# A new opening order with halved weight loads, a column-group mean square, and row additions of the first FFN stage moved ahead

## The chip, the cores and the metric

The kernel runs on one core of a Trainium2 chip. The core has a matrix engine (TensorE, PE in the profile; PEld is its weight load), a vector engine (VectorE, DVE), a scalar engine (ScalarE, ACT), GpSimd (POOL) and SyncE (SP), which here only issues transfers. Each engine works through its own list of instructions in order and waits on semaphores for the others. On-chip memory is SBUF; matmuls write PSUM. The metric is the device time of one execution in microseconds; less is better.

## What is computed

A decoder trunk of two layers over 512 tokens of width 1024. Each layer is a half-step SwiGLU FFN, a token mixer and a second half-step FFN, each behind an RMS norm that is modulated by adaLN columns computed from `c`:

```python
c_act = jax.nn.silu(c)
for l in range(DEPTH):
    mod = (c_act @ w_ada[l] + b_ada[l]).reshape(B, N_MOD, D_MODEL)
    sh1, sc1, gt1, sh2, sc2, gt2, sh3, sc3, gt3 = [mod[:, i, None, :] for i in range(N_MOD)]
    hn = rms_norm(h, g_ffn1[l]) * (1.0 + sc1) + sh1
    h = h + 0.5 * (1.0 + gt1) * swiglu(hn, w_ffn1_in[l], w_ffn1_out[l])
    ...
```

All inputs are float32. The kernel splits each large operand into a high part (rounded to the fast matmul format fp32r) and a low part (the rest), and forms a product as three matmuls: high x high, high x low, low x high.

## The kernel before

**Layout.** The residual `h` lies in SBUF transposed: eight row blocks k = 0 to 7 of 128 features by 512 tokens. A weight tile is 128 output features by 1024 inputs, 512 KB; for output tile n the pair wH, wL (high, low) is made from the raw tile by a copy on ACT and a subtraction on DVE (`split`, L136 to L141; in the opening L1430 and L1432). An output tile of the FFN's input side takes 8 row blocks x 3 matmuls of 128x512 = 24 (`mm3`, L123 to L129).

**The opening** (`begin`, L1317) computes the first norm and its modulation and, interleaved with them, the first six output tiles (n = 0 to 5, gate and up of three pairs) of the first FFN. It runs in a pool of its own, `first`, which holds the adaLN streams (`wada`, 4 buffers of 1 MB), the raw weights (`wfirst`), the scaled rows `z`, and the pairs of tiles 4 and 5; the pairs of tiles 0 to 3 lie in the pool `wp`, which all stages share. Nearly all its instructions are pinned (`pin`, L1324): each engine takes them in the order in which `PLAN` (L33) is walked. A word of `PLAN` is one step:

- `R`: the reciprocal root mean square spread over all partitions (PE); `z`k: h[k] times it (DVE).
- `ada`k, `part`k, `col`k, `gm`k: the scale and shift columns of row block k from stream k, on PE; `d`k and `e`k: the same as two dot products on DVE (L1394), each followed by a read of the accumulator, and `gm`.
- `x`k: z[k] scaled and shifted (ACT, L1422); `H`k and `L`k: high and low part of the normed row block, hnH on ACT, hnL on DVE (L1424, L1426).
- `wH`n, `wL`n: the pair of weight tile n. `W`n: n matmuls on ones whose result nobody reads (warm-up).
- `P`nk and a letter: one large matmul of tile n and row block k (L1409): `a` high weight x hnH, `b` high weight x hnL, `c` low weight x hnH.

The loads of the opening go out on SP in the order of the calls of `fetch` (a stream of 1 MB) and `fetch_w` (a weight tile); `more` (L1396) adds calls after some steps, as buffers come free. Before the plan, ACT and DVE square the eight row blocks, DVE adds the squares in seven steps (L1375), and PE sums over partitions (L1380).

**The first stage** (`ffn`, L350) uses the pool `act`, which takes the place of `first` in SBUF once that is closed. `projector` (L305) yields the opening's six tiles and computes ten more, n = 6 to 15, each with a freshly loaded pair; raw weights have two buffers (`wraw`), pairs four. Of each gate and up tile ACT takes silu, DVE multiplies (L522), ACT and DVE split the result into actH and actL (L523, L524). Meanwhile DVE forms further adaLN columns as dot products with `crep` (silu(c) on all partitions, which the opening writes to memory and this stage loads, L203), and prepares the second half of the stage, which uses a Strassen-like scheme over pairs (`pair_in`): `whole(n)` (L394) adds hnH and hnL of four row blocks back to full values, four additions of 128x512 into tiles `x` of the pool `act`; `combine` (L402) makes the sums P1, P2, T3, T4 of them. `late` (L500) says behind which of the stage's sixteen tiles each of these six steps is put. Apart from the pins a scheduler places the instructions of an engine by the order in which they are written and by when their inputs are ready; `queue_behind(name)` (L133) puts an instruction behind the one kept under that name in the order of its engine.

Of the kernel before, what the change touches and what calls it, by code (L numbers as in the profile page):

```python
# [17 lines left out]
P = 128  # L18
# [14 lines left out]
PLAN = """  # L33
ada0 R0 part0 s0 col0 z0 wH0 ada1 gm0 z5 x0 z4 part1 z1 H0 W2 col1 z7 s1 P00a wH1 gm1 z3 x1 L0 W4 P10a ada2 z6 wH2 z2 H1 P00b wL2 P10b P20a part2 P20b
P01a wH3 col2 L1 P20c P11a gm2 P30a P30b wL3 x2 P01b P11b P21a P21c H2 P21b d3 P31a P30c P31b P31c P02a P12a L2 P22a P22c P32a e3 P02b P12b P22b wH4
P32c P32b wL0 W1 P40a x3 P40b P41a P41b P42a H3 P42b d4 P00c P01c P02c P03a P03c L3 P13a wH5 P23a P23c P33a e4 P03b P13b P50a P50b P51a P51b P52a wL5
x4 P52b P23b P33c P33b H4 P43a d5 P43b P50c P51c P52c P53a P53b L4 P53c P04a P04c e5 P14a P04b P14b P24a P24c P24b P34a P34c wL4 x5 P34b P44a P44b
P54a H5 P54c d6 P54b P40c P41c P42c P43c P44c L5 P05a P05c P15a e6 P05b P15b P25a P25c P25b P35a P35c wL1 P35b x6 P45a P45c P45b P55a H6 P55c d7 P10c
P11c P12c P13c P14c P15c L6 P55b P06a P06c e7 P06b P16a P16c P16b P26a P26c P26b x7 P36a P36c P36b P46a H7 P46c P46b P56a P56c L7 P56b P07a P07c P07b
P17a P17c P17b P27a P27c P27b P37a P37c P37b P47a P47c P47b P57a P57c P57b  # L40
""".split()
GROUPS = ((0, 12), (12, 22))
STEP = 0.65
# [25 lines left out]
def trunk_kernel(ctx, tc, ins, out, layers=L, phases=("ffn1", "mix", "ffn2")):  # L69
# [280 lines left out]
    def ffn(l, w_in, w_pair, w_out, hn, im, ss, need, then, first, ready, coming):  # L350
# [6 lines left out]
        with tc.tile_pool(name="act", bufs=1) as ap_:  # L357
# [36 lines left out]
            def whole(n):  # L394

                for k in (2 * n, 2 * n + 4):
                    x = ap_.tile([P, 2, T], F32, name="x", tag="act", bufs=12)
                    for i in range(2):
                        tt(x[:, i], *(t.bitcast(F32) for t in hn[k + i]), ALU.add)
                    rows_.append(x)  # L400

            def combine(name):  # L402
# [108 lines left out]
            for g, (j0, j1) in enumerate(GROUPS):  # L511
                for p in range(j0 // 2, j1 // 2):
                    if p < n_first:
                        X = new_x(p)
                        for j in (2 * p, 2 * p + 1):
# [4 lines left out]
                            act(pg.like(s), pg.view, AF.Silu)  # L520
                            for seen, part in pu.pieces(s):
                                stt(part, part, -1.0, seen, ALU.mult, ALU.mult)  # L522
                            nc.scalar.copy(xs[j][0], s)  # L523
# [793 lines left out]
    def begin(pool):  # L1317
# [12 lines left out]

        wa, wf = [], []

        def fetch():
            w = pool.tile([P, 2 * D], F32, name="wada", tag="wada", bufs=4)
            nc.sync.dma_start(w, ins["wa0"][len(wa)])
            wa.append(w)

        def fetch_w():
            j, g = divmod(len(wf), 2)
            w = pool.tile([P, KD, P], F32, name="wfirst", tag="wfirst", bufs=5)  # L1340
            nc.sync.dma_start(w, ins["w1i"][0, j, g])
            wf.append(w)

# [15 lines left out]
        for k in range(KD):  # L1359
            pin("PE", mm(turned[k // 4][:, k % 4], cT[:, k : k + 1].to_broadcast([P, P]), cst("ident"), start=True, stop=True))  # L1360
        warm(22)
        ss, sqs = new_ss(), {}
        sqs[0] = ss
        for i in range(KD):
            if i in (3, 4):
                x = pool.tile([P, T], F32, name="sqs", tag=f"sq{i}")
            else:
                x = E("sq") if i else ss
            sqs[i] = x
            if i == 3:  # L1370
                pin("DVE", tt(x, h[i], h[i], ALU.mult))
            else:
                pin("ACT", act(x, h[i], AF.Square))
        for a, b in ((0, 1), (0, 2), (0, 3), (4, 5), (4, 6), (4, 7), (0, 4)):
            pin("DVE", tt(sqs[a], sqs[a], sqs[b], ALU.add))  # L1375
        for f in (fetch, fetch_w, fetch, fetch_w, fetch_w, fetch, fetch_w, fetch):
            f()
        pt = psum([P, NB], "ps_ss")
        for b in range(NB):
            pin("PE", mm(pt[:, b : b + 1], ss[:, b * P : (b + 1) * P], ones[:, :1], start=True, stop=True))  # L1380
        r = pool.tile([P, NB], F32, name="rstd_t", tag="rstd_t")
        pin("ACT", act(r, pt, AF.Sqrt, bias=vals["eps"], scale=1.0 / D))
        pin("DVE", nc.vector.reciprocal(r, r))
        rstd = psum([P, T], "ps_rstd", "r1")
        pin("DVE", stt(col["gb"], bsc, 1.0, g1, ALU.add, ALU.mult))
        zs, ws, part, sums, pts = {}, {}, {}, {}, {}

        def finish(c, sc, sh):
            pin("DVE", stt(col["gm0"][:, c], sc, g1[:, c], col["gb"][:, c], ALU.mult, ALU.add))
            pin("DVE", tt(col["sh0"][:, c], sh, bsh[:, c], ALU.add))  # L1390

# [3 lines left out]

        more = {"ada0": (fetch, fetch_w), "ada1": (fetch,), "wL0": (fetch_w, fetch), "e3": (fetch,)}  # L1396

        def step(token):
            kind = "P" if token[0] == "P" else token.rstrip("0123456789")
            k = token[len(kind) :]  # L1400
            if kind == "W":
                return warm(int(k))
            if kind == "P":
                n, k, p = int(k[0]), int(k[1]), "abc".index(k[2])
                if n not in pts:
                    pts[n] = psum([P, T], "ps_mm", ("r0", "r1", "mm")[n % 3])
                w, x = ws[n][p == 2][:, k], weave(hn[k][p == 1])
                first, last = (token == ends[n][e] for e in range(2))
                latest["large"] = pin("PE", mm(paired(pts[n]), w, x, start=first, stop=last, skip_group_check=True))  # L1409
                return  # L1410
            k = int(k)
            c = slice(k, k + 1)
            if kind == "R":
                for b in range(NB):
                    pin("PE", mm(rstd[:, b * P : (b + 1) * P], r[:, b : b + 1].to_broadcast([P, P]), cst("ident"), start=True, stop=True))
            elif kind == "s":
                pin("ACT", act(crep[:, k * 512 : k * 512 + 512], turned[k].rearrange("p k n -> p (k n)"), AF.Silu))
            if kind == "z":
# [6 lines left out]
            elif kind == "L":  # L1425
                pin("DVE", nc.vector.tensor_sub(hn[k][1], zs[k], hn[k][0].bitcast(F32)))  # L1426
            elif kind == "wH":
                home, bufs = (wp, 4) if k < 4 else (pool, 2)
                ws[k] = tuple(home.tile([P, KD, P], F32R, name=x, tag=x, bufs=bufs) for x in ("wH", "wL"))
                pin("ACT", nc.scalar.copy(ws[k][0], wf[k]))  # L1430
            elif kind == "wL":
                pin("DVE", nc.vector.tensor_sub(ws[k][1], wf[k], ws[k][0].bitcast(F32)))  # L1432
            elif kind == "ada":
# [11 lines left out]
            elif kind == "gm":  # L1445
                finish(c, sums[k][:, :1], sums[k][:, 1:])
            elif kind == "d":
                dot(k, "sc", 0)
            elif kind == "e":
                dot(k, "sh", D)  # L1450
                finish(c, col["sc"][:, c], col["sh"][:, c])
            for f in more.get(token, ()):
                f()

# [41 lines left out]
def lay_out(i):  # L1496
# [11 lines left out]
    streams = first.transpose(3, 1, 0, 2, 4).reshape(KD, P, 2 * D)  # L1508
    a["wa0"] = c(np.concatenate([streams[:3], wT[0, 1::-1, 3:].transpose(1, 2, 0, 3).reshape(5, P, 2 * D)]))
    for n, w in (("w1", "w_ffn1_in"), ("w2", "w_ffn2_in")):  # L1510
# [66 lines left out]
```

## Time and profile before

| | us |
|---|---|
| median of three runs (1805.30 to 1809.03) | 1805.43 |
| the profiled execution, whole | 1807.22 |
| its span, first to last instruction | 1805.5 |
| PE busy in the span | 1774.8 |
| DVE busy | 1350.3 |
| ACT busy | 840.9 |

All times of the profile count from the start of the span. The page gives totals and the costliest groups of instructions. The other views are answers from the same trace: the busy time of each engine by stretches, the timeline of an engine (start, duration, engine, line, operation, output<-inputs, count; in brackets how long the engine was idle before it and what ended that), the waits by pairs, and the transfers by issuing line. A timeline row with a count above 1 is a merged run of alike instructions.

### The profile page before, as it was taken

The page shows a single profiled execution, that of the slowest core. Times are in us where ns is not written, and L with a number is a line of the kernel's source. Part 1 is how long each engine was busy: PE and PEld are TensorE (multiplying, and loading weights), DVE is VectorE, ACT ScalarE, POOL GpSimd, SP SyncE. Part 2 cuts the span into 40 slices and gives each one's busy share as a digit, 9 for nine tenths or more (in the row PEclk, how much of TensorE's full clock was granted, in tenths as well). Part 3 has the DMA queues.
Part 4 walks back from the last instruction along what each step waited for, and adds up shares of the span by engine and source line. Part 5 has one row for each costly group of instructions (what it writes and reads, how often), then busy time and mean ns, then how long its engine had stood idle before and what let it go on. Part 6 is the DMA issues. An engine that isn't in the chain of part 4 may idle for free.

```text
span 1805.5 us, 33687 instructions
## 1 busy us (share of the span) xinstructions
PE 1774.8 (98%) x13848; PEld 1616.9 (90%) x13848; DVE 1350.3 (75%) x2187; ACT 840.9 (47%) x1295; POOL 142.5 (8%) x227
## 2 busy tenths in 40 slices
PE   8999999999999999999999999999999999999999
PEld 6889899987778999899899989999876798999998
DVE  6688587877767977677888776887686788864862
ACT  5353255374443554255355524544654345533541
POOL 0101010101000001100100020110000000010000
PEclk9999999999999999999999999999999999999999
DMA  8667876623123576967737687773421427684742
GB/s 342 218 176 232 243 201 197 228 65 103 54 88 120 150 200 193 291 181 206 246 108 200 180 290 204 195 231 105 122 73 32 141 79 198 186 245 132 198 141 71
DMA packets 91405, 309.93 MB, mean 172 GB/s; under 512 B 10417, under 2 KB 11185, under 8 KB 90225
## 3 DMA queue, kind: packets, MB, share of 16 engines
q1 hardware_dynamic: 61920, 201.58, 32.9%
q0 software_dynamic: 29328, 106.18, 23.5%
q8 instruction: 109, 1.79, 0.4%
q14 instruction: 48, 0.39, 0.1%
HBM read 303.79 MB, written 3.93 MB: 170 GB/s over the span
## 4 chain that ended last, share of the span: by engine, by line
PE 81%; DVE 9%; DMA 4%; ACT 4%; issue 3%; POOL 0%; SPq 0%; ACTq 0%; DVEq 0%; POOLq 0%
PE ps_mm L127 13%; PE ps_mm L128 13%; PE ps_mm L129 13%; PE ps_d L431 7%; PE ps_d L433 7%; PE ps_d L432 7%; PE ps_f L433 3%; PE ps_f L431 3%; PE ps_f L432 3%; PE ps_g L433 2%; PE ps_g L431 2%; PE ps_g L432 2%; DVE wL L141 2%; PE ps_mm L1409 1%; ACT wH L139 1%
## 5 line engine op out<-in xcount | busy, mean ns | idle before, releaser
L139 ACT CAST wH<-wraw 128x1024 fp32r<-128x1024 f32 (+2 forms) x290 | 263.9, 916 | 465.8 <-PE ps_mm L128 212.4
L141 DVE TENSOR_TENSOR wL<-wraw,wH 128x1024 fp32r<-128x1024 f32 (+2 forms) x290 | 305.5, 1058 | 123.3 <-ACT wH L139 122.0
L127 PE MATMUL ps_mm<-actH,wH 128*128 128x512 f32 (+1 forms) x784 | 281.0, 358 | 0.0
L129 PE MATMUL ps_mm<-actH,wL 128*128 128x512 f32 (+1 forms) x784 | 280.6, 358 | 0.3 <-DVE wL L141 0.3
L128 PE MATMUL ps_mm<-actL,wH 128*128 128x512 f32 (+1 forms) x784 | 280.5, 358 | 0.0
L127 PE MATMUL ps_mm<-hnH,wH 128*128 128x512 f32 (+1 forms) x712 | 246.8, 353 | 1.7 <-ACT hnH L289 1.3
L128 PE MATMUL ps_mm<-hnL,wH 128*128 128x512 f32 (+1 forms) x712 | 246.2, 348 | 0.1
L129 PE MATMUL ps_mm<-hnH,wL 128*128 128x512 f32 (+1 forms) x712 | 244.8, 346 | 0.6 <-DVE wL L141 0.6
L431 PE MATMUL ps_d<-comH,wH 128*128 128x256 f32 x816 | 225.2, 276 | 0.8 <-ACT s L457 0.7
L432 PE MATMUL ps_d<-comL,wH 128*128 128x256 f32 x816 | 224.4, 275 | 0.0
L433 PE MATMUL ps_d<-comH,wL 128*128 128x256 f32 x816 | 224.4, 275 | 0.0
L141 DVE TENSOR_TENSOR wL<-sum,wH 128x1024 fp32r<-128x1024 f32 x102 | 124.9, 1225 | 81.0 <-ACT wH L139 80.8
L197 DVE SCALAR_TENSOR_TENSOR wada<-wada,crep 128x1024 f32<-128x1024 f32 x128 | 153.2, 1219 | 29.2 <-DMA wada<-in_wadaT 28.9
L129 PEld LDWEIGHTS ps_mm<-actH,wL 128*128 128x128 f32 x784 | 148.7, 190 | 17.5 <-DVE wL L141 0.7
L127 PEld LDWEIGHTS ps_mm<-actH,wH 128*128 128x128 f32 x784 | 148.7, 190 | 16.8 <-ACT wH L139 0.2
L128 PEld LDWEIGHTS ps_mm<-actL,wH 128*128 128x128 f32 x784 | 148.7, 190 | 16.6
L431 PEld LDWEIGHTS ps_d<-comH,wH 128*128 128x128 f32 x816 | 156.6, 192 | 2.3 <-ACT s L457 2.3
L433 PEld LDWEIGHTS ps_d<-comH,wL 128*128 128x128 f32 x816 | 156.7, 192 | 0.0
L432 PEld LDWEIGHTS ps_d<-comL,wH 128*128 128x128 f32 x816 | 156.6, 192 | 0.0
L139 ACT CAST wH<-sum 128x1024 fp32r<-128x1024 f32 x102 | 106.8, 1047 | 104.6 <-PE ps_f L432 42.4
L127 PEld LDWEIGHTS ps_mm<-hnH,wH 128*128 128x128 f32 x712 | 133.1, 190 | 22.0 <-issue 7.9
L129 PEld LDWEIGHTS ps_mm<-hnH,wL 128*128 128x128 f32 x712 | 135.4, 190 | 14.0 <-DVE wL L141 1.0
(389 smaller groups left out, 3861.0 us busy)
## 6 DMA issues: line engine op xcount, KB each, us to landing
wada<-in_wadaT POOLq DMA_DIRECT2D x128, 512.0 KB, 4.8
wraw<-in_wmi SPq DMA_DIRECT2D x40, 512.0 KB, 3.6
wraw<-in_w2p SPq DMA_DIRECT2D x36, 512.0 KB, 3.8
wraw<-in_w1p SPq DMA_DIRECT2D x32, 512.0 KB, 4.3
wraw<-in_w1o SPq DMA_DIRECT2D x32, 384.0 KB, 4.4
wraw<-in_w2o SPq DMA_DIRECT2D x32, 384.0 KB, 4.6
wraw<-in_w1o SPq DMA_DIRECT2D x32, 320.0 KB, 3.7
wraw<-in_w2o SPq DMA_DIRECT2D x32, 320.0 KB, 3.4
```

The lines of the kernel that those rows point to most:

```text
L127: mm(acc, wH, xH, start=start, stop=False)
L128: mm(acc, wH, xL, start=False, stop=False)
L129: latest["large"] = mm(acc, wL, xH, start=False, stop=stop)
L139: nc.scalar.copy(hi, src)
L141: return nc.vector.tensor_sub(lo, src, hi.bitcast(F32))
L197: stt(w, w, 1.0, crep, ALU.mult, ALU.mult, accum_out=out_)
L431: mm(acc, wH, xH, start=start and i + k == 0, stop=False, skip_group_check=True)
L432: mm(acc, wH, xL, start=False, stop=False, skip_group_check=True)
L433: mm(acc, wL, xH, start=False, stop=k == 3, skip_group_check=True)
L1409: latest["large"] = pin("PE", mm(paired(pts[n]), w, x, start=first, stop=last, skip_group_check=True))
```

## The change

It rewrites the opening and touches the first stage in three places.

1. Each raw weight tile of the opening is loaded and split in two halves of 256 KB (row blocks 0 to 3, and 4 to 7); `wH` and `wL` become steps on a half (`wH1a`, `wL1a`, ...). `fetch` takes a word, and all opening loads are pinned on SP. `wfirst` has six buffers.
2. The silu of `c` is taken before it is spread; `crep` is a plain copy. The squares are summed by PE as they are made: for each row block four matmuls with a 32-column weight of ones, each into its own group of 32 partitions. Of 28 warm-up matmuls ahead of the plan's, 22 go and 8 come.
3. Scale and shift columns are finished on ACT instead of DVE. Stream 2 moves from PE (`ada2`, `part2`, `col2`) to DVE (`d2`, `e2`).
4. `PLAN` is new; the host lays stream 2 out for the dot products.
5. `whole(0)` is called at the start of the stage and its last addition kept as "sums"; wL of tile 6 and the products of the first three pairs are queued behind it. `whole(1)` is put behind tile 1, and the four sums two tiles earlier than before.

```diff
 PLAN = """
-ada0 R0 part0 s0 col0 z0 wH0 ada1 gm0 z5 x0 z4 part1 z1 H0 W2 col1 z7 s1 P00a wH1 gm1 z3 x1 L0 W4 P10a ada2 z6 wH2 z2 H1 P00b wL2 P10b P20a part2 P20b
...
+R0 ada0 z2 wH1a z0 wH3a z6 part0 z7 W2 col0 wL1a gm0 x0 z1 W3 ada1 wL3a H0 z3 wH5a P10a P10c P30a z5 part1 P30c wH0a P50a wL5a col1 wH2a P00a L0 P50c
+gm1 P20a wL2a x1 P00b P10b P20b wL0a P20c H1 P30b P50b d2 P00c P01a P01c P11a P11c L1 P21a P21c P31a wH4a e2 P01b P11b P21b P31c P31b z4 P51a gm2 P51c
+x2 P51b wL4a P40a P40b P41a d3 H2 P40c P41b P41c P02a P02c P12a e3 P12c P22a P22c P32a P32c L2 gm3 P42a P42c x3 P52a d4 P02b P12b P22b H3 P32b P42b e4
...
+P55a x6 P55c wL2b P05b P15b d7 P25b H6 P24c P25c P35b P45b P55b L6 P06a P16a P16c e7 P06b P16b P26a P26c P26b wL0b gm7 P36a P36b x7 P46a wL3b P04c
+P05c P06c H7 P34c P35c P36c L7 P46c P46b P56a P56c P56b P07a P07c P07b P17a P17c P17b P27a P27c P27b P37a P37c P37b P47a P47c P47b P57a P57c P57b
 """.split()
+HALF = {"a": slice(0, KD // 2), "b": slice(KD // 2, KD)}
+BANK = ("r0", "r0", "mm", "r1", "r1", "mm")
...
-            places = {3: ("norm_act", "norm_dve"), 4: ("act", "dve")} if ready else {}
+            places = {3: ("norm_act", "norm_dve"), 4: ("act", "dve")} if ready else {6: (None, "sums")} if pts else {}
...
-            late = ((1, 0), (3, 1), (4, "P1"), (5, "P2"), (6, "T3"), (7, "T4"))
+            late = ((1, 1), (10, "P1"), (11, "P2"), (12, "T3"), (13, "T4"))
             early = ((0, 0), (3, 1), (3, "P1"), (4, "P2"), (5, "T3"), (5, "T4"))
-            when = [(8 + m, n) for m, n in late] if n_first == 4 else early
+            when = late if n_first == 4 else early
+            if n_first == 4:
+                latest["sums"] = whole(0)
...
-                            for seen, part in pu.pieces(s):
-                                stt(part, part, -1.0, seen, ALU.mult, ALU.mult)
+                            with queue_behind("sums" if n_first == 4 and j < 3 else None):
+                                for seen, part in pu.pieces(s):
+                                    stt(part, part, -1.0, seen, ALU.mult, ALU.mult)
...
+        def fetch(token):
+            n = int(token[1])
+            if token[0] == "a":
+                w = wa[n] = pool.tile([P, 2 * D], F32, name="wada", tag="wada", bufs=4)
+                pin("SP", nc.sync.dma_start(w, ins["wa0"][n]))
+            else:
+                if n not in wf:
+                    wf[n] = pool.tile([P, KD, P], F32, name="wfirst", tag="wfirst", bufs=6)
+                pin("SP", nc.sync.dma_start(wf[n][:, HALF[token[2]]], ins["w1i"][0, n // 2, n % 2][:, HALF[token[2]]]))
...
+        pss = psum([P, P], "ps_ss")
+        sqs = {}
         for i in range(KD):
+            sqs[i] = pool.tile([P, T], F32, name="sqs", tag="z", bufs=KD)
+            if i in (3, 5, 7):
+                pin("DVE", tt(sqs[i], h[i], h[i], ALU.mult))
             else:
+                pin("ACT", act(sqs[i], h[i], AF.Square))
+            for b in range(NB):
+                pin("PE", mm(pss[32 * b : 32 * b + 32], ones[:, :32], sqs[i][:, b * P : (b + 1) * P], start=i == 0, stop=i == KD - 1))
...
+        for token in "a0 w1a w3a a1 w5a w0a w2a a2 w4a a3".split():
+            fetch(token)
+        warm(5)
...
         def finish(c, sc, sh):
-            pin("DVE", stt(col["gm0"][:, c], sc, g1[:, c], col["gb"][:, c], ALU.mult, ALU.add))
-            pin("DVE", tt(col["sh0"][:, c], sh, bsh[:, c], ALU.add))
+            pin("ACT", act(col["gm0"][:, c], sc, AF.Identity, bias=col["gb"][:, c], scale=g1[:, c]))
+            pin("ACT", act(col["sh0"][:, c], sh, AF.Identity, bias=bsh[:, c]))
...
-        more = {"ada0": (fetch, fetch_w), "ada1": (fetch,), "wL0": (fetch_w, fetch), "e3": (fetch,)}
+        more = {"ada0": "a4 w5b", "ada1": "a5 w4b w1b w2b", "e2": "a6 w3b w0b", "e3": "a7"}
...
+            if kind in ("wH", "wL"):
+                n, part_ = int(k[0]), HALF[k[1]]
+                if n not in ws:
+                    home, bufs = (wp, 4) if n < 4 else (pool, 2)
+                    ws[n] = tuple(home.tile([P, KD, P], F32R, name=x, tag=x, bufs=bufs) for x in ("wH", "wL"))
+                wH, wL, w = (x[:, part_] for x in (*ws[n], wf[n]))
```

`fetch`, `warm` and `whole` are as shown or described above; `BANK` names the PSUM banks of the six tiles.

More of the change, by code (lines that the diff above doesn't have):

```diff
@@ L398, in whole @@
                     for i in range(2):
-                        tt(x[:, i], *(t.bitcast(F32) for t in hn[k + i]), ALU.add)
+                        last_ = tt(x[:, i], *(t.bitcast(F32) for t in hn[k + i]), ALU.add)
                     rows_.append(x)
+                return last_
             def combine(name):
@@ L1329, in pin @@
             return m
[L1331 to L1342, printed above, removed]
+        wa, wf = {}, {}
+        def fetch(token):
[7 more added lines that the diff above has]
+                pin("SP", nc.sync.dma_start(wf[n][:, HALF[token[2]]], ins["w1i"][0, n // 2, n % 2][:, HALF[token[2]]]))
         pw = psum([P, T], "ps_warm", "mm")
@@ L1359, in begin @@
         for k in range(KD):
[L1360 to L1363, printed above, removed]
+            pin("PE", mm(turned[k // 4][:, k % 4], cact[:, k : k + 1].to_broadcast([P, P]), cst("ident"), start=True, stop=True))
+        pss = psum([P, P], "ps_ss")
+        sqs = {}
         for i in range(KD):
-            if i in (3, 4):
-                x = pool.tile([P, T], F32, name="sqs", tag=f"sq{i}")
-            else:
[L1368 to L1382, printed above, removed]
+            sqs[i] = pool.tile([P, T], F32, name="sqs", tag="z", bufs=KD)
@@ L1383, in begin @@
+            if i in (3, 5):
+                warm((i - 1) // 2)
+        for token in "a0 w1a w3a a1 w5a w0a w2a a2 w4a a3".split():
+            fetch(token)
+        warm(5)
+        r = pool.tile([P, P], F32, name="rstd_t", tag="rstd_t")
+        pin("DVE", stt(col["gb"], bsc, 1.0, g1, ALU.add, ALU.mult))
+        pin("ACT", act(r, pss, AF.Sqrt, bias=vals["eps"], scale=1.0 / D))
         pin("DVE", nc.vector.reciprocal(r, r))
         rstd = psum([P, T], "ps_rstd", "r1")
-        pin("DVE", stt(col["gb"], bsc, 1.0, g1, ALU.add, ALU.mult))
@@ L1426, in step @@
                 pin("DVE", nc.vector.tensor_sub(hn[k][1], zs[k], hn[k][0].bitcast(F32)))
[L1427 to L1432, printed above, removed]
             elif kind == "ada":
@@ L1450, in step @@
                 dot(k, "sh", D)
-                finish(c, col["sc"][:, c], col["sh"][:, c])
-            for f in more.get(token, ()):
-                f()
+            for load in more.get(token, "").split():
+                fetch(load)
         ends = {n: [[t for t in PLAN if t[:2] == f"P{n}"][e] for e in (0, -1)] for n in range(6)}
```

28 lines of the change are left out of this document (15 added, 13 removed).

## The prediction

> **What bounds the kernel now.** I read the page first, then the waits and the table of busy time by stretches for the first 120 us, then the timeline of each engine around every gap that these show. The change touches only those 120 us; what follows keeps its instructions.
>
> ```profile
> span 1805.5 us, 33687 instructions
> ## 1 busy us (share of the span) xinstructions
> PE 1774.8 (98%) x13848; PEld 1616.9 (90%) x13848; DVE 1350.3 (75%) x2187; ACT 840.9 (47%) x1295; POOL 142.5 (8%) x227
> ```
>
> TensorE (PE) is busy for 98% of the span, so time can only be won where it waits or runs at a lower clock. In the opening it does both:
>
> ```profile
> 32.00:36.00 4.00, 3.03 (x15) 2.30 (x13) 2.29 (x7) 0.40 (x1) 0.00 (x0) 1.00 1.01 416
> 36.00:40.00 4.00, 2.67 (x7) 2.19 (x8) 2.69 (x4) 2.38 (x3) 0.00 (x0) 0.71 1.01 399
> ```
>
> Columns: stretch and its length, busy us of PE, weight loads, VectorE (DVE), ScalarE (ACT) and POOL, then the granted PE clock, the DMA share and GB/s. The DMA engines are full (1.01, about 416 GB/s) while PE is not: the opening waits for its loads in the order in which they come. The timeline has the places:
>
> ```profile
> 22.75 1.07 PE L1437 MATMUL ps_ada<-wada,cz 128*32 128x256 f32 x16 [1.46 <-DMA wada<-in_wa]
> ...
> 37.33 0.52 PE L1409 MATMUL ps_mm<-hnH,wH 128*128 128x512 f32 x1 [2.31 <-ACT wH L1430]
> ...
> 41.06 0.38 PE L1409 MATMUL ps_mm<-hnH,wH 128*128 128x512 f32 x1
> ...
> 52.07 0.38 PE L1409 MATMUL ps_mm<-hnL,wH 128*128 128x512 f32 x1
> ...
> 59.84 0.38 PE L1409 MATMUL ps_mm<-hnL,wH 128*128 128x512 f32 x1
> ```
>
> The third adaLN stream lands at 22.75; the last weight tile is so late that PE idles 2.31 us before 37.33. The opening's 144 large matmuls end with the one at 59.84. At full clock one takes (59.84 - 52.07) / 36 = 0.216 us. The first nine from 37.33 take 3.73 us up to 41.06 instead of 1.94: after the idle 2.31 us PE runs at half clock, and that loses 1.8 us more.
>
> **The opening, part by part.** Call T the time at which the first matmul behind the opening could start; now T = 59.84 + 0.22 = 60.06. Useful work is 144 x 0.216 = 31.1 us.
>
> *Loads.* Six weight loads become twelve halves; the bytes stay 11 MB.
>
> ```profile
> wada<-in_wa SPq DMA_DIRECT2D x8, 1024.0 KB, 12.6
> wfirst<-in_w1i SPq DMA_DIRECT2D x6, 512.0 KB, 11.8
> ```
>
> Ahead of the third stream, a2, now stand two streams and three whole weight tiles, in the new order two streams and five halves: 0.25 MB less, 0.6 us at 416 GB/s. So a2 lands at 22.1 instead of 22.75. What matters more is that halves of five weight tiles are there by then, where now PE waits for a whole one until 37.33. The trace shows no load of 2 KB per partition in this queue. Bounds: no loss, or one fifth less rate on the 1.25 MB ahead of a2, 0.8 us; I take none, since the present 4 KB and 8 KB rows together already fill the engines.
>
> The Trainium skill (DMA: Bandwidth & Descriptors, "Measured (HBM→SBUF, 128 partitions, SWDGE, issued from GpSimd)") speaks against halving: it has 1 MB transfers at 341 GB/s and asks for batches of 1 MB. By that figure a2 would land an estimated 0.7 us later, and T with it. The trace has 416 GB/s for a mix of 0.5 and 1 MB loads that queue up behind each other, so I do not use it.
>
> *The mean square.* The seven row additions on DVE go; 32 column-group matmuls on PE take their place, beside the arriving x.
>
> ```profile
> 8.50 1.90 ACT L1373 ACTIVATE sq<-h 128x512 f32<-128x512 f32 x3
> ...
> 12.49 1.05 PE L1380 MATMUL ps_ss<-ones_r,ss 128*128 128x1 f32 x8 [0.18 <-DVE ss L1375]
> ...
> 15.67 0.69 DVE L1420 TENSOR_TENSOR z<-h,ps_rstd 128x512 f32<-128x512 f32 x1 [1.56 <-PE ps_rstd L1415]
> ```
>
> The squares end at 10.40, the sum is used at 12.49, the first z starts at 15.67. With the additions gone the tail of 15.67 - 12.49 = 3.2 us starts at 10.4 plus at most one such group of matmuls (0 to 1.05 us): z at 13.6 to 14.7. Before d2, the first dot product of a2, the new order puts 13 DVE steps of 0.60 us (next rows), 7.8 us: 21.4 to 22.5, against a2 at 22.1. So this costs 0 to 0.4 us; I take 0. Were z not earlier at all (15.67), d2 would start at 23.5 and T be 1.4 later.
>
> *The chain that sets T.* Durations:
>
> ```profile
> 42.68 1.22 DVE L1394 SCALAR_TENSOR_TENSOR wada<-wada,crep 128x1024 f32<-128x1024 f32 x1
> 43.83 0.08 DVE L1394 DVE_READ_ACCUMULATOR wada<-wada,crep 128x1 f32 x1
> 43.83 0.69 DVE L1426 TENSOR_TENSOR hnL<-z,hnH 128x512 fp32r<-128x512 f32 x1
> 44.43 1.22 DVE L1394 SCALAR_TENSOR_TENSOR wada<-wada,crep 128x1024 f32<-128x1024 f32 x1
> ```
>
> ```profile
> 5.16 0.29 ACT L1357 ACTIVATE sh<-cact,v_eps 128x1 f32<-128x1 f32 x1
> ...
> 45.90 0.81 ACT L1422 ACTIVATE z<-z,sh,gm 128x512 f32<-128x512 f32 x1 [2.77 <-DVE sh L1390]
> 46.74 0.62 ACT L1424 CAST hnH<-z 128x512 fp32r<-128x512 f32 x1
> ```
>
> On DVE a dot product holds the engine 1.15 us and a 512-column step 0.60. From a2 at 22.1: d2, L1, e2 are 1.15 + 0.60 + 1.3 = 3.05; gm2, now two 128x1 steps on ACT, at most 2 x 0.29; x2 0.81; H2 0.62: row 2 of the normed input is ready at 27.2. The order has 36 matmuls before the first that needs it (7.8 us of work after H0 and H1, so PE waits there) and 108 from it on: T = 27.2 + 108 x 0.216 = 50.5. Two checks that nothing later binds. DVE from d2: 12 dots (13.8) and 15 steps of 0.60 (9.0) end at 44.9, and 23 matmuls (5.0 us) follow the last of them, L7: 49.9. The last stream, a7 (1 MB, 2.5 us), lands behind what PE's weights now wait for (36.2, as 37.33 follows the cast), at 38.7, and its dots come at about 40 anyway. gm on ACT costs ACT 8 x 0.58 us, hidden in an engine that is 47% busy. The warm-up matmuls lie ahead of the wait for H2; if the clock were half there, 36 matmuls would take 15.5 us instead of 7.8, up to 3 us late. So the opening gives 60.06 - 50.5 = **9.6 us** (7 to 10.5).
>
> **The row additions.** They write tiles of the stage's pool, and that pool lies in the memory of the opening's pool. What the first writes into it wait for, the trace shows:
>
> ```profile
> 58.10 1.22 DVE L141 TENSOR_TENSOR wL<-wraw,wH 128x1024 fp32r<-128x1024 f32 x1 [5.79 <-ACT wH L139]
> ...
> 59.25 1.96 DVE L522 SCALAR_TENSOR_TENSOR silu<-silu,ps_mm 128x512 f32<-128x512 f32 x3
> ...
> 60.29 0.33 SPq L203 DMA_DIRECT2D crep<-silu_c  x1
> 60.36 0.62 ACT L523 CAST actH<-silu 128x512 fp32r<-128x512 f32 x1
> ```
>
> The load of crep and the first actH start at 60.29 and 60.36, just behind the end of the opening's last matmul (59.84 + 0.38 = 60.22), though the first of the three products, actH's data, was done a third of 1.96 us behind 59.25, at 59.9. The last two weight pairs that those matmuls read are in the opening's pool. So the first addition cannot run in DVE's idle time ahead of T (now 52.3 to 58.1); it starts at T + 0.2. And the change queues two things behind all four additions: the wL of weight tile 6, which now is ready before T (58.10 + 1.22 = 59.3), and three products. Four additions (4 x 0.60) and wL end at T + 0.2 + 2.4 + 1.22 = T + 3.8. Tile 6's third matmul needs wL at T + 0.43: PE waits **3.4 us**. Behind that on DVE stand three products, three actL and the other four additions, 10 x 0.60 = 6.0 us, and then wL of tile 7: done between T + 5.0 (taken first) and T + 11.1 (last). Tile 7 wants it at T + 3.4 + 24 x 0.216 + 0.43 = T + 9.0. If the clock also halves after the wait, as after 2.31 us now (1.8 us), PE is there at T + 10.8. Both together make the loss 3.4 to 5.5; I take **5.5**, the end that the emission order and the row at 37.33 favour.
>
> The Trainium skill (TensorE: Matmul & The Clock Gate, "HAM oscillation — how this bites in real kernels") forbids idle gaps over about 3.4 us; by that the 3.4 us wait stands on the edge. The trace already loses the clock after 2.31 us, and this decides.
>
> **What comes back.** With DVE rid of 4.8 us of additions before the stage's end, its last waits should go:
>
> ```profile
> 118.45 0.38 PE L433 MATMUL ps_g<-hnH,wL 128*128 128x256 f32 x1 [0.84 <-DVE wL L141]
> ...
> 119.88 0.38 PE L431 MATMUL ps_d<-comH,wH 128*128 128x256 f32 x1 [0.72 <-ACT s L457]
> ```
>
> That is 0.84 + 0.72 = 1.56 us; I take 1.5 (0 to 1.56).
>
> **Sum:** -9.6 + 5.5 - 1.5 = -5.6 us. It is made against the profiled execution, span 1805.5, whole time 1807.2, which lies 1.8 above the median of 1805.43. Taken from the median: 1799.8. About 0.2%, 3.6 us, is what a measurement here can tell from no change.
>
> **The rivals.**
>
> *The additions do run ahead of T.* Then nothing waits: -9.6 - 1.5 = -11.1, 1794.3. For it: L7 ends some 5 us before T, and the four additions need 2.4. Against it: the two rows at 60.29 and 60.36. Chance 0.22.
>
> *The opening's gain is half eaten.* Cold clock ahead of 27 (3 us) or z no earlier (1.4), with the 5.5 us loss and nothing coming back: -9.6 + 3 + 5.5 = -1.1, 1804.3. For it: fewer warm-up matmuls. Chance 0.15.
>
> *Slower: DVE becomes the bound of the first stage.* There are two buffers for raw weights, so the load of tile n+2 starts when wL of tile n is done. That round is now covered by two tiles of PE, 48 x 0.216 = 10.4 us. If each wL, pushed back behind additions and dot products that wait for their own loads, makes the round 4 us longer than that, tiles 8 to 15 lose 4 us per pair: 4 x 4 = 16 on top of 3.4, against 11.1 won: +8, 1813. It decides from about 2 us per pair on (8 + 3.4 > 11.1). Against it: DVE is 75% busy, and the added work is moved, not new. Chance 0.13.
>
> **How the numbers follow.** The forecast has 0.50 and its own range, 1797 to 1802.5 (loss of 3.4 to 5.5, opening 7 to 10.5). Faster by over 0.2%, below 1801.8: 0.47 of it, the 0.22 and 0.02 of the half-eaten case, 0.71. Within 0.2%: 0.03 of it, 0.12 of the half-eaten and 0.01 of the last case, 0.16. Slower: 0.12 of the last and 0.01 of the half-eaten, 0.13. The range from 1793.5 to 1807 leaves out a little of the first rival and most of the last.
>
> **What would show it.** T at 50 to 51, no PE idle over 1 us after 20, clock near 1.00 throughout 28 to 50: the opening. The first addition of hnH and hnL right behind the last opening matmul, then wL, and PE waiting about 3.4 us on it in tile 6: the loss. Additions at 45 to 48 would show the first rival; waits of PE on wL in tiles 8 to 15 the last. No wait at ps_g and ps_d of the first pair: what comes back. I am wrong if T is above 53, or if the waits behind T add to less than 2 us.

## The result, and the profile after

| | median us (runs) | lowest to highest |
|---|---|---|
| before | 1807.24 (14) | 1804.52 to 1809.65 |
| after | 1806.01 (14) | 1804.90 to 1811.13 |

The ratio after to before is 1.0001, 95% interval 0.9994 to 1.0008: **no change**. (The two medians differ by 1.2 us, less than the runs of either kernel scatter.) The forecast was 0.3% faster. The opening ends 9.5 us earlier, as forecast; what it wins is lost again in the next 20 us. Of e6 and e9 below one run each, near 2270 us at a clock of 0.75, is left out of every figure.

The page of the changed kernel, its span and the busy time of its engines:

```profile
span 1803.5 us, 33740 instructions
...
PE 1769.9 (98%) x13868; PEld 1611.8 (89%) x13868; DVE 1349.0 (75%) x2176; ACT 845.3 (47%) x1314; POOL 142.5 (8%) x227
```

Its busy time by stretches (columns as in the prediction: PE busy first; third from the end the granted PE clock, then DMA share and GB/s):

```profile
20.00:40.00 20.00, 19.98 (x91) 16.63 (x91) 19.45 (x34) 15.21 (x31) 0.00 (x0) 1.00 1.02 412
40.00:60.00 20.00, 16.91 (x76) 13.69 (x74) 14.29 (x24) 8.97 (x14) 2.29 (x4) 1.00 0.49 181
60.00:80.00 20.00, 14.35 (x56) 11.95 (x57) 11.58 (x18) 5.72 (x7) 2.12 (x4) 0.83 0.59 204
80.00:100.00 20.00, 20.00 (x95) 17.51 (x94) 18.63 (x29) 9.04 (x11) 2.26 (x3) 1.00 0.76 211
100.00:120.00 20.00, 20.00 (x119) 18.23 (x118) 14.28 (x15) 9.09 (x13) 0.84 (x1) 1.00 0.61 173
```

The opening itself is as it should be: from 20 to 40 PE is busy for 19.98 of 20 us at full clock, where before it was 2.67 of 4 in the worst stretch. The hole is new and lies between 50 and 72. PE's timeline there, all its waits, between the last matmul of the opening and the first whole stretch behind:

```profile
50.30 0.38 PE L1412 MATMUL ps_mm<-hnL,wH 128*128 128x512 f32 x1
50.52 0.46 PE L129 MATMUL ps_mm<-hnH,wH 128*128 128x512 f32 x1
...
52.40 0.48 PE L129 MATMUL ps_mm<-hnH,wH 128*128 128x512 f32 x1 [1.21 <-ACT wH L141]
54.46 0.48 PE L131 MATMUL ps_mm<-hnH,wL 128*128 128x512 f32 x1 [1.37 <-DVE wL L143]
62.75 0.48 PE L129 MATMUL ps_mm<-hnH,wH 128*128 128x512 f32 x1 [3.27 <-ACT wH L141]
66.35 0.79 PE L131 MATMUL ps_mm<-hnH,wL 128*128 128x512 f32 x1 [2.90 <-DVE wL L143]
```

PE's list takes two matmuls of the next tile ahead of those that still lack their `wL`. So the four waits are for the cast of tile 7, `wL` of tile 6, the cast of tile 8 and `wL` of tile 7. The third costs nothing by itself, since `wL` of tile 7 comes 3.6 us later still. DVE's timeline says why the two `wL` are late:

```profile
50.77 2.50 DVE L401 TENSOR_TENSOR x<-hnH,hnL 128x512 f32<-128x512 f32 x4 [5.04 <-PE ps_mm L1412]
53.19 1.22 DVE L143 TENSOR_TENSOR wL<-wraw,wH 128x1024 fp32r<-128x1024 f32 x1
54.32 1.88 DVE L528 SCALAR_TENSOR_TENSOR silu<-silu,ps_mm 128x512 f32<-128x512 f32 x3
56.12 0.68 DVE L530 TENSOR_TENSOR actL<-silu,actH 128x512 fp32r<-128x512 f32 x1
56.72 2.49 DVE L401 TENSOR_TENSOR x<-hnH,hnL 128x512 f32<-128x512 f32 x4
59.13 0.68 DVE L530 TENSOR_TENSOR actL<-silu,actH 128x512 fp32r<-128x512 f32 x1
59.73 1.22 DVE L199 SCALAR_TENSOR_TENSOR wada<-wada,crep 128x1024 f32<-128x1024 f32 x1
...
60.87 1.22 DVE L199 SCALAR_TENSOR_TENSOR wada<-wada,crep 128x1024 f32<-128x1024 f32 x1
...
63.25 0.69 DVE L530 TENSOR_TENSOR actL<-silu,actH 128x512 fp32r<-128x512 f32 x1 [1.15 <-ACT actH L529]
...
63.93 1.22 DVE L199 SCALAR_TENSOR_TENSOR wada<-wada,crep 128x1024 f32<-128x1024 f32 x1
...
65.08 1.22 DVE L143 TENSOR_TENSOR wL<-wraw,wH 128x1024 fp32r<-128x1024 f32 x1
```

Between the two `wL`, of tile 6 at 53.19 and of tile 7 at 65.08, stand three products, three `actL`, four additions and three adaLN dot products. In the third `actL` DVE itself waits, for ACT; and ACT stands behind the cast of tile 8, which waits for its load. The timelines of SP, POOL and ACT, in that order:

```profile
54.43 0.33 SPq L303 DMA_DIRECT2D wraw<-in_w1i  x1
```
```profile
51.38 1.58 POOL L210 DMA_DIRECT2D wada<-in_wadaT  x3 [4.63 <-ACT silu L525]
```
```profile
61.65 1.04 ACT L141 CAST wH<-wraw 128x1024 fp32r<-128x1024 f32 x1 [5.35 <-DMA wraw<-in_w1i]
62.61 0.61 ACT L529 CAST actH<-silu 128x512 fp32r<-128x512 f32 x1
```

The load of tile 8 goes out when `wL` of tile 6 has freed its buffer (54.43), behind three adaLN streams, and is there 7.2 us later. Before, that load went out ahead of the streams and its cast ran 3.5 us later, as its own timelines of SP, POOL and ACT show. In the kernels below it is the same: issued ahead of the streams, the load is followed by its cast within 3.6 us (e5, e9), and issued behind them only after 6.6 to 7.3 (e2, e3, e10).

```profile
59.36 0.33 SPq L301 DMA_DIRECT2D wraw<-in_w1i  x1
```
```profile
60.92 1.59 POOL L208 DMA_DIRECT2D wada<-in_wadaT  x3 [7.59 <-ACT silu L520]
```
```profile
62.85 1.05 ACT L139 CAST wH<-wraw 128x1024 fp32r<-128x1024 f32 x1 [0.82 <-DMA wraw<-in_w1i]
```

**One measure for all kernels.** From T on, every kernel here runs the same number of matmuls (13580) in nearly one order. So one can take the time at which the n-th matmul behind the opening starts, less the same time in the trace of before; below, this difference is called the lead, and a negative one means earlier. For the changed kernel this lead is 50.52 - 60.06 = -9.54 us at n = 0, -6.36 at 12, +2.09 at 36, +2.35 from 48 to 288, and 121.18 - 120.65 = +0.53 at 300, behind the place of the two old waits. So: opening -9.5, tiles 6 to 8 +11.9, the old waits -1.8, sum +0.5. The span is 2.0 us shorter than before since the trace gains another 2.3 us far behind, in code that the change doesn't touch. There the trace of before has two stretches at half clock, at 498 and 1382, that this trace lacks, worth about 1.6 us each; waits elsewhere take 1.0 back. Traces of other kernels below differ from before by as much, both ways, at the same places. I take it as scatter.

### The profile page after: what moved, and what is told of

Same layout as the page of the kernel before. It is cut to its first block, busy times and chain, and to the rows that moved or that the text cites. A ratio compares the mean times of both kernels' runs of the same rounds, so it can differ in the third digit from the quotient of the medians.

```text
span 1803.5 us, 33740 instructions
## 1 busy us (share of the span) xinstructions
PE 1769.9 (98%) x13868; PEld 1611.8 (89%) x13868; DVE 1349.0 (75%) x2176; ACT 845.3 (47%) x1314; POOL 142.5 (8%) x227
## 4 chain that ended last, share of the span: by engine, by line
PE 79%; DVE 8%; DMA 6%; issue 3%; ACT 3%; POOL 0%; SPq 0%; ACTq 0%; POOLq 0%; DVEq 0%
PE ps_mm L129 12%; PE ps_mm L130 12%; PE ps_mm L131 12%; PE ps_d L434 7%; PE ps_d L436 7%; PE ps_d L435 7%; PE ps_f L436 3%; PE ps_f L435 3%; PE ps_f L434 3%; DMA wada<-in_wadaT 2%; PE ps_mm L1412 2%; DVE wL L143 2%; PE ps_g L436 2%; PE ps_g L435 2%; PE ps_g L434 2%
## 5 line engine op out<-in xcount | busy, mean ns | idle before, releaser
L129 PEld LDWEIGHTS ps_mm<-hnH,wH 128*128 128x128 f32 x712 | 133.6, 191 | 27.2 <-issue 7.6
```

The costliest lines, as they stand in the source:

```text
L129: mm(acc, wH, xH, start=start, stop=False)
```

## The experiments

The first theory: the additions start only behind the opening's last matmul, because their tiles' pool lies on the opening's; the two orders behind them then hold up `wL`. The rival: the earlier T alone uncovers DVE work and loads, wherever the additions stand.

The results together. "Tiles 6 to 8" is the lead at matmul 72 less that at 0, "old waits" from 72 to 300. The leads are of one trace each and hold what was lost at half clock there.

| kernel | lead at T | tiles 6 to 8 | old waits | lead at 300 | ratio to before, 95% interval |
|---|---|---|---|---|---|
| after | -9.5 | +11.9 | -1.8 | +0.5 | 1.0001 (0.9994 to 1.0008) |
| e1_open | -9.6 | +2.1 | +0.6 | -6.9 | 0.9975 (0.9962 to 0.9988) |
| e2_adds | -0.6 | +12.8 | -1.8 | +10.3 | 1.0050 (1.0036 to 1.0065) |
| e3_early_w7 | -9.0 | +3.9 | -0.5 | -5.6 | 0.9973 (0.9959 to 0.9987) |
| e4_ahead | -9.7 | +1.7 | -1.8 | -9.8 | 0.9943 (0.9924 to 0.9962) |
| e5_no_queue | -10.1 | +3.2 | -1.8 | -8.7 | 0.9963 (0.9951 to 0.9976) |
| e6_kept_rows | -9.7 | +1.9 | -1.8 | -9.6 | 0.9957 (0.9944 to 0.9969) |
| e7_kept_early | -9.1 | +0.1 | -1.8 | -10.8 | 0.9953 (0.9941 to 0.9965) |
| e8_whole_loads | -6.8 | +4.0 | -1.7 | -4.6 | 0.9988 (0.9977 to 0.9999) |
| e9_products_queued | -10.1 | +9.7 | -1.8 | -2.2 | 1.0011 (1.0001 to 1.0020) |
| e10_w6_queued | -9.6 | +7.3 | -1.8 | -4.1 | 0.9972 (0.9962 to 0.9982) |
| e11_table_early | -9.8 | 0.0 | -1.8 | -11.6 | 0.9938 (0.9926 to 0.9950) |

**e1_open: the opening alone.** The first stage of before behind the new opening.

```diff
-            late = ((1, 1), (10, "P1"), (11, "P2"), (12, "T3"), (13, "T4"))
+            late = ((1, 0), (3, 1), (4, "P1"), (5, "P2"), (6, "T3"), (7, "T4"))
-            when = late if n_first == 4 else early
+            when = [(8 + m, n) for m, n in late] if n_first == 4 else early
-            if n_first == 4:
-                latest["sums"] = whole(0)
```

The two orders behind "sums" go as well.

> The new opening with the first stage as before: no addition ahead, nothing queued behind one. Theory A (the additions are kept behind the opening's last matmul by the pool, and the two weight steps queued behind them are what PE waits for): T at 50.5 as in the changed kernel, no PE wait over 0.5 us in tiles 6 to 8, the two waits of 0.84 and 0.72 us ahead of ps_g and ps_d still there; 9 to 10 us less than before. Theory B (DVE and the DMA engines of the first stage need the time, so an earlier T only moves the wait there; tile 8's raw weight took 7.2 us to land beside the adaLN streams): PE waits on weights of tile 8 or 9 all the same, and no more than 3 us are won.

The runs win 4.5 us (2.2 to 6.9), the trace 6.9 up to matmul 300: neither the 9 to 10 of A nor the 3 at most of B. The 11.9 us shrink to 2.1, so the additions and their orders make nearly all of them. But PE's timeline has a wait that theory A did not have, and the two old waits are longer than before (together 2.19 instead of 1.56):

```profile
63.25 0.48 PE L131 MATMUL ps_mm<-hnH,wL 128*128 128x512 f32 x1 [1.77 <-DVE wL L143]
```
```profile
111.58 0.38 PE L436 MATMUL ps_g<-hnH,wL 128*128 128x256 f32 x1 [1.47 <-DVE wL L143]
113.01 0.38 PE L434 MATMUL ps_d<-comH,wH 128*128 128x256 f32 x1 [0.72 <-ACT s L460]
```

DVE's timeline names the first one, `wL` of tile 8 behind dot products whose streams are late:

```profile
56.93 1.23 DVE L199 SCALAR_TENSOR_TENSOR wada<-wada,crep 128x1024 f32<-128x1024 f32 x1 [2.27 <-DMA wada<-in_wadaT]
...
61.98 1.22 DVE L143 TENSOR_TENSOR wL<-wraw,wH 128x1024 fp32r<-128x1024 f32 x1
```

So the rival has a true core, of about 2 us.

**e2_adds: the first stage's changes alone**, with the opening of before.

> The old opening with the three changes to the first stage. Theory A: the same waits behind T = 60.1 as in the changed kernel behind its T (about 3 us on wL of tile 6, about 8.7 us with the slow clock around wL of tile 7), less the 1.8 us that come back before the pairs: 8 to 11 us slower than before. Theory B (the loss comes from the earlier T): at most 3 us slower.

+12.8 in tiles 6 to 8 and -1.8 at the old waits: 0.5% slower. The loss doesn't come from the early T; it is in the additions' place and the orders behind them, and comes with either opening.

**e3_early_w7: tile 7 ahead.**

```diff
-... hn, BANKS[:3], first, 1, ready)
+... hn, BANKS[:3], first, 2 if n_first == 4 else 1, ready)
```

> The changed kernel, but the pair of weight tile 7 is emitted ahead of the products, so that its subtraction stands right behind that of tile 6 on DVE, ahead of four additions and three dot products. Theory A: the wait on wL of tile 6 stays at 3.1 us, that of 66.35 goes, a smaller one on wL of tile 8 may take its place; the loss falls from 11.9 to between 3.1 and 5.5, so 6 to 8 us less than before. Theory B: PE waits for tile 8's load instead, the total stays within 2 us of the changed kernel.

The wait on tile 7 goes and with it 8 us; a smaller one on tile 8 comes (1.39 us at 66.12). Theory A holds. The lead of -5.6 is a little short of the 6 to 8, since the cast of tile 7 now stands ahead of the silus on ACT, and PE waits for the PSUM banks these free (0.75 and 0.28 us), and since the old waits came back only by 0.5: 0.35 us at ps_g and 0.72 at ps_d remain, although the additions stand where the change put them. Why they remain is open.

**e4_ahead: the additions before T.** Their tiles lie in a pool of their own that is opened ahead of the opening's; it holds the squares, then `z`, then the sums, then the results of pairs 4, 5 and 10, so it takes no memory that wasn't taken. The additions are also put behind the opening's last subtraction (`queue_behind("opened")`, not shown).

```diff
+    xp = own.enter_context(tc.tile_pool(name="kept", bufs=1))
...
-                zs[k] = pool.tile([P, T], F32, name="z", tag="z", bufs=KD)
+                    pairs[k // 2] = xp.tile([P, 2, T], F32, name="z", tag="x", bufs=4)
+                zs[k] = pairs[k // 2][:, k % 2]
...
-                    x = ap_.tile([P, 2, T], F32, name="x", tag="act", bufs=12)
+                    x = xp.tile([P, 2, T], F32, name="x", tag="x", bufs=4) if n_first == 4 else ...
```

> The changed kernel with the additions' tiles in a pool of their own beside the opening's (it holds the squares and the scaled rows first, then the sums, then the results of pairs 4 and 5), and the additions put behind the opening's last subtraction. Theory A: the first additions run from 45.7 on, wL of tile 6 is done by T = 50.5, PE does not wait in tiles 6 to 8, and the 1.8 us before the pairs come back too: 10.5 to 11.5 us less than before. Theory B: the additions run ahead of T, yet PE still waits 3 us or more in tiles 7 and 8.

DVE's timeline: five additions, then `wL` of tile 6, all before T:

```profile
45.53 3.10 DVE L405 TENSOR_TENSOR x<-hnH,hnL 128x512 f32<-128x512 f32 x5
48.53 1.22 DVE L143 TENSOR_TENSOR wL<-wraw,wH 128x1024 fp32r<-128x1024 f32 x1
```

The two orders of the change are still in this kernel, and the one that is new can only hold the additions back. What lets them start 5 us earlier is the pool, and PE waits 1.4 us in all instead of 8.8: the pool is the cause that the orders need. The 1.4 us are those on tile 8 again (theory A had none).

**e5_no_queue, e9_products_queued, e10_w6_queued: the two orders.** The changed kernel without either (both edits below), with the one on the products only (the first edit), and with the one on `wL` of tile 6 only (the second).

```diff
-            places = ... else {6: (None, "sums")} if pts else {}
+            places = ... else {}
...
-                            with queue_behind("sums" if n_first == 4 and j < 3 else None):
+                            with queue_behind(None):
```

> The changed kernel without its two orders behind the additions (wL of tile 6, the three products). Theory A (it is DVE's order behind T): wL of tile 6 runs at 48.5 to 49.7 and PE does not wait in tile 6; the additions still start only at 50.8, because of the pool, and stand with two products ahead of wL of tile 7, which is done at about 58.6 where tile 7 wants it at 56.2: a wait of about 2.4 us, 0.5 more in tile 8, with or without 1.8 us of slow clock. Loss 2.4 to 5, total 6.4 to 9 us less than before. Rival (the orders are the whole loss): no wait over 0.5 us behind T, 11 us less.

> The changed kernel, but only the three products are queued behind the additions, not wL of tile 6. wL of tile 6 runs before T and PE does not wait in tile 6. On DVE wL of tile 7 again stands behind three products, three halves of their results, eight additions and three dot products, as in the changed kernel: done at about 64 where tile 7 wants it at 56.6, a wait of 7 us and some 2 us of slow clock behind it. Loss behind T about 9, total 1 to 3 us less than before. If wL of tile 6 is the larger part of the loss instead, it falls below 5 us.

> The changed kernel, but only wL of tile 6 is queued behind the additions, not the products. PE waits about 3.1 us on wL of tile 6 as in the changed kernel. wL of tile 7 is done at about 60, some 6 us earlier than there; but the raw weight of tile 8 is again asked for only when wL of tile 6 is done (54.4) and lands at about 61.6 beside the streams, and two of its matmuls stand ahead of tile 7's rest: a wait of 3 us on wH of tile 8. Loss 6 to 8.5, total 3 to 5.5 us less than before. If the load of tile 8 does not matter, the second wait is under 1 us and the total 7 us less.

PE's timelines: e5 has 2.16 us (forecast 2.4), e9 has 7.17 (forecast 7):

```profile
58.42 0.48 PE L131 MATMUL ps_mm<-hnH,wL 128*128 128x512 f32 x1 [2.16 <-DVE wL L143]
```
```profile
63.46 0.79 PE L131 MATMUL ps_mm<-hnH,wL 128*128 128x512 f32 x1 [7.17 <-DVE wL L143]
```

The loss in tiles 6 to 8 is 3.2 us without orders, 9.7 with that on the products, 7.3 with that on `wL`, and 11.9 with both. So they aren't additive, but either alone costs more than everything else. The products' order was the one that I had counted as three steps of 0.60: it changes where the scheduler puts all the rest, and `wL` of tile 7 slips behind the dot products. In e10 the wait on tile 8 is 1.01 us, not 3; the load lands at 61.3 as expected, but PE gets there later, since the clock fell behind a wait of 1.66 us (below). The runs of e9 are 2 us slower than before where its lead is -2.2; its trace too has given that lead back by the end (span 1805.9). It loses 1.9 us around a stretch at half clock at 583 that before lacks and 2.4 more between 700 and 1000, and wins 1.6 at 1382. Its runs had less clock as well: a mean of 0.9953, against 0.9977 for before on that chip. What lowers it is open.

**e6_kept_rows, e7_kept_early, e11_table_early: no additions at all.** `z` of the opening, scaled and shifted, already is what hnH + hnL gives back. If it stays, in a pool of its own as in e4, the eight additions go, and the two orders with them.

```diff
-            rows_, sums = [], {}
+            rows_, sums = list(kept_rows) if n_first == 4 else [], {}
...
+        kept_rows.extend(pairs[k] for k in (0, 2, 1, 3))
```

e7 adds `3 if n_first == 4` in the place of e3's 2, and e11 a silu of one column as the opening's last step on ACT:

```diff
+        pin("ACT", act(col["sh0"][:, :1], cact[:, :1], AF.Silu))
```

> The new opening, and no row additions in the first stage at all: the scaled rows z, which already are the full values, stay in a pool of their own until the sums are made, and the results of pairs 4, 5 and 10 take their place. Nothing is queued behind anything. Theory A: no PE wait in tiles 6 and 7, the wait on wL of tile 8 behind three dot products stays (1.4 to 1.8 us, as in the two runs with the new opening and no wait in tiles 6 and 7), the waits before the pairs go: 9.5 to 10.5 us less than before. Rival (the additions' place does not matter once they are off the path): as in the run with the additions ahead of T, within 1 us, which this would not tell apart from A; a result more than 2 us from it speaks against both.

> As e6_kept_rows, and the pairs of tiles 7 and 8 are emitted ahead of the products, so that wL of tile 8 stands ahead of the dot products on DVE. If those dot products, late with their streams, are what makes PE wait in tile 8, that wait goes too: no PE wait over 0.5 us between 20 and 120, and 11 to 12 us less than before. If tile 8's load is too late beside the streams, PE waits there still, and the total is that of e6_kept_rows.

> e7_kept_early with one more step at the opening's end on ACT, a silu of one column, so that the table load of 1.28 us falls into ACT's idle time before 47.4 instead of ahead of the first silu. In e7_kept_early the first matmul behind the opening waited 0.75 us for that silu to free its PSUM bank; this wait should go: T at 50.3 and no PE wait over 0.3 us between 20 and 120, 0.7 us less than e7_kept_early by the trace. If ACT still comes late because of the cast of tile 7, the wait stays at 0.4 us or more.

e6 keeps the wait on tile 8 (1.52 us), as forecast. In e7, 10.8 us ahead by the trace and 8.5 (6.3 to 10.7) by the runs, it is gone: the dot products with their late streams were its cause. A new one stands at T, on a silu that has yet to free its bank, because the cast of tile 7 and a table load are now ahead of the silus on ACT:

```profile
50.97 0.48 PE L129 MATMUL ps_mm<-hnH,wH 128*128 128x512 f32 x1 [0.75 <-ACT silu L526]
```

With the table loaded in ACT's idle time, that goes too. The stretches of e11:

```profile
20.00:40.00 20.00, 20.00 (x92) 16.98 (x92) 20.00 (x36) 15.27 (x31) 0.00 (x0) 1.00 1.03 411
40.00:60.00 20.00, 20.00 (x94) 17.51 (x93) 13.25 (x21) 11.90 (x19) 2.29 (x4) 1.00 0.56 213
60.00:80.00 20.00, 20.00 (x94) 17.52 (x93) 15.78 (x24) 6.96 (x9) 2.64 (x5) 1.00 0.84 281
80.00:100.00 20.00, 20.00 (x95) 17.50 (x94) 18.70 (x26) 9.16 (x12) 2.09 (x3) 1.00 0.77 217
100.00:120.00 20.00, 20.00 (x169) 19.54 (x168) 14.12 (x16) 11.97 (x15) 1.87 (x3) 1.00 0.67 163
```

PE is busy for 100.00 of 100 us at full clock. e11 has the lowest time, 0.62% less than before (median 1795.16 us; before on that chip 1806.00). By the runs it cannot be told from e4, whose interval holds it; the traces put it 1.8 us ahead of e4 at matmul 300.

**e8_whole_loads: are the halves worth anything?** e1_open with whole loads.

```diff
-                pin("SP", nc.sync.dma_start(wf[n][:, HALF[token[2]]], ...))
+                if token[2] == "a":
+                    pin("SP", nc.sync.dma_start(wf[n], ins["w1i"][0, n // 2, n % 2]))
```

> As e1_open, but each weight tile of the opening is loaded whole where its first half was; the steps and their order stay. Ahead of the third adaLN stream then stand 1.25 MB more, 3.1 us at the 400 to 416 GB/s of the trace: the first dot product at 25.2 instead of 22.1, T at 53.5 instead of 50.5, and the total 3 us above e1_open. If the order of the plan is what gains and not the halves, T stays within 1 us of 50.5.

The first dot product of the third stream starts at 24.82 instead of 22.03, both from DVE's timeline:

```profile
24.82 1.23 DVE L1396 SCALAR_TENSOR_TENSOR wada<-wada,crep 128x1024 f32<-128x1024 f32 x1 [0.54 <-DMA wada<-in_wa]
```
```profile
22.03 1.23 DVE L1395 SCALAR_TENSOR_TENSOR wada<-wada,crep 128x1024 f32<-128x1024 f32 x1
```

T comes 2.8 us later. So the halves carry 2.8 of the opening's 9.6 us, through the place of one stream. The other 6.8 belong to the rest of the new opening (its order, the mean square, stream 2 on DVE), which was not taken apart. The 2.8 instead of the 3.1 worked out leave 0.3 us that the halves may cost, within the 0 to 0.8 of the prediction. The old waits are gone here too (-1.7), although the additions stand where before had them.

## Why the prediction was wrong

**The opening: right.** a2's first dot product starts at 22.11 (predicted 22.1), row 2 is ready at 26.92 (27.2), z starts at 13.37 (13.6 to 14.7, so 0.2 ahead of the range), T is 50.52 (50.5). One detail was off: PE doesn't wait for row 2. The 36 matmuls ahead of it and the chain end together, so T was set by both, and that they meet is luck. For the chain speaks e8, where the third stream comes 2.8 us later, and T with it. ACT's and DVE's rows:

```profile
26.30 0.62 ACT L1436 CAST hnH<-z 128x512 fp32r<-128x512 f32 x1
```
```profile
22.11 1.23 DVE L1397 SCALAR_TENSOR_TENSOR wada<-wada,crep 128x1024 f32<-128x1024 f32 x1 [0.54 <-DMA wada<-in_wa]
```

**Where the additions start: right.** Predicted T + 0.2, measured 50.77, released by the opening's last matmul. e4 shows that it is the pool.

**Tile 6: right.** `wL` was predicted to end at T + 3.8 and ends at 54.41, T + 3.9; the loss is 3.2 us of 3.4. (PE spends it in two waits, of 1.21 and 1.37 us, with two matmuls of tile 7 between them.)

**Tile 7: the step that failed.** "Behind that on DVE stand three products, three actL and the other four additions, 10 x 0.60 = 6.0 us, and then wL of tile 7: done between T + 5.0 (taken first) and T + 11.1 (last)." It is done at 65.08 + 1.22 = 66.30, T + 15.8, outside my own bounds. The list was short by the three dot products that the scheduler also put ahead (3 x 1.15) and by the 1.15 us in which DVE waited for the third actH, which on ACT stood behind the cast of tile 8, and so behind a load that I had not followed: 3.45 + 1.15 = 4.6, and 11.1 + 4.6 = 15.7. The bound was no bound. I had taken "last" to mean behind the work that the change moves, but an instruction pushed back in a list that a scheduler writes can fall behind anything that is ready in its model, dot products included. PE then waited 3.27 and 2.90 us, and lost 2.1 more at half clock. The loss was 11.9 us, not 5.5.

**What comes back: right in size**, 1.82 us (1.5, at most 1.56). The reason given, that DVE is rid of the additions there, is not borne out: e3 is rid of them and keeps 1.07 us of these waits, and e8 has them where before did and loses the waits. So the size is right by luck, and what makes these waits stays open.

With 11.9 for 5.5, and 1.8 for 1.5, my own sum is -9.5 + 11.9 - 1.8 = +0.6. The likeliest case had the sign of every term, and the mechanism of the first two; one term was too small by 6.4 us, more than the whole gain. I had put a chance on the opening's gain being half eaten, at the wrong place, and the slower rival (tiles 8 to 15 short of weights) did not occur: there is no wait in 80 to 120.

## What to carry to other kernels

An order edge that holds an instruction back isn't priced by the instructions in front of it alone: price what else can get in between, up to the first thing that depends on another queue, and follow each engine there (here DVE, ACT, SP and the streams on POOL's queue). Work can be moved into an engine's idle time only if its destination is free then; here a pool laid over another's memory waited for that pool's last reader, and moving the tile was worth more than moving the instruction. Not doing the work at all was worth as much (a lead of -9.6 in e6, -9.8 in e4): the values that the eight additions made had been in memory, and keeping them cost no byte more.

## What the runs showed of the hardware

**The clock falls for stretches of a fixed beat.** In these traces the half clock comes in stretches of 3.41 us, or two of them in a row; only the kernel's end cuts one. In before they start at 37.64, 498.44 and 1382.50; the distances, 460.80 and 884.06 us, are 135 and 259 times 3.413, so the beat runs on through the kernel. Where it lies against the kernel differs from one execution to the next. The half clock behind T follows a stretch in which PE waited. In e10 a wait of 1.66 us lies whole in one stretch of the beat; PE is busy for 1.72 us of it, and the next stretch has half the clock:

```profile
52.28:55.69 3.41, 1.72 (x7) 1.21 (x8) 3.41 (x5) 0.50 (x1) 0.60 (x2) 1.00 0.87 314
55.69:59.10 3.41, 3.41 (x10) 2.69 (x9) 3.41 (x7) 0.00 (x0) 0.00 (x0) 0.50 0.95 363
```

In the changed kernel, the wait of 1.37 us at the same place is cut by the beat at 53.37, no stretch there has PE busy for less than 1.93 us, and the clock stays at 1.00. Then the pair of 3.27 and 2.90 us leaves PE almost idle for two stretches, and two at half clock follow, from 63.61 to 70.44:

```profile
60.20:63.61 3.41, 0.70 (x2) 0.30 (x2) 2.26 (x5) 1.96 (x3) 1.06 (x2) 1.00 0.23 88
63.61:67.03 3.42, 0.68 (x2) 0.59 (x3) 3.42 (x6) 0.10 (x1) 0.53 (x1) 0.50 0.72 249
```

The Trainium skill (TensorE: Matmul & The Clock Gate, "HAM oscillation — how this bites in real kernels") warns of idle gaps over about 3.4 us. No gap of e10 is half as long, and the clock fell. The measurement decides: a wait of 1.7 us can be enough, if it falls into one stretch. It need not be: e1's wait of 1.77 us leaves PE busy for 1.67 us of the stretch from 59.81 to 63.22, and the clock stays at 1.00. What decides so near the edge is not shown, and idle time is not all that counts: far behind, in e3, a stretch at half clock from 580.83 follows one with PE busy for 2.49 of 3.41 us.

The runs scatter with the clock that they were granted. Of the changed kernel's 14, the three with a mean of 0.994 took 1809.8 to 1811.1 us, and the six with 0.998 took 1805.0 to 1806.1.

**A table load costs its own time here and no more.** ACT's timeline of e7:

```profile
49.03 1.28 ACT L526 ACT_TABLE_LOAD   x1
50.32 1.57 ACT L526 ACTIVATE silu<-ps_mm 128x512 f32<-128x512 f32 x3
```

The Trainium skill (ScalarE: Activation LUTs, "What ACT_TABLE_LOAD costs") has 1.28 us for the load, as here, and 1.38 us of drain with it. Here the load starts 0.02 us behind the cast before it (47.02 + 1.99 = 49.01), and the silu 0.01 us behind the load; no such drain shows.
